# Weights laid out by the host so that each partition reads one contiguous run

## The chip, the cores and the metric

The kernel runs on one core of a Trainium2 chip. The metric is the device time of one execution in microseconds (us); what the host does before the launch is not in it. A core has TensorE (matmuls, "PE" in the rows, "PEld" for its weight loads), VectorE (DVE), ScalarE (ACT), GpSimd (POOL) and SyncE (SP), which issues most DMAs. Sixteen DMA engines serve all queues of the core.

## The reference, cut to what matters

Two layers of a diffusion backbone over 256 latent and 256 context tokens of width 1024, all in fp32. Each layer has a modulated input projection into three token mixers, a merge and a layer norm, then a mixture of 64 experts with eight per token and a shared expert, and a second layer norm.

```python
h = x * (1.0 + m[1]) + m[0]                      # m from s_c @ w_mod[l] + b_mod[l]
q, k, v, lx, lg, z, xbc, dt, gates = split(h @ w_in)   # 1024 x 7184
...
proj = einsum('blnk,nkd->blnd', ys, w_branch)    # three branches, 512 x 1024 each
out  = einsum('blnd,de->ble', g * proj, w_out)   # 1024 x 1024
x = layer_norm(DN_ALPHA * x + m[2] * mix, ln1_g[l], ln1_b[l])
...
# each of 64 experts e, on the tokens routed to it:
swiglu(h_pad[toks], w_up[e], w_down[e]) * ws     # w_up 1024 x 512, w_down 256 x 1024
```

The last layer needs the latent tokens only. The expert weights are 3 MB per expert, 192 MB per layer.

## The kernel before, in words

The kernel keeps 20 named slots of 1 MB in SBUF (8 KB in each of 128 partitions) and streams all weights through them in chunks of at most 1 MB. The contraction dimension is cut into blocks `k` of 128 rows; row `p` of each block goes to partition `p`. A chunk is therefore loaded with a view `(k p) f -> p k f`: each partition gets, for each `k`, one row piece of the matrix. The length of that piece in HBM is 1 KB for `w_mod`, `w_in` and `w_out` (256 columns of wider rows), 2 KB for `w_up` and `ws_up` (a full row of 512), 4 KB for `w_down` and `ws_down` (a full row of 1024), 512 B for `w_branch` (128 columns) and 256 B for the router weights and the lru blocks.

All these loads are issued by SP in program order, and a load waits until its slot is free. The order of the instructions is made while the program is built: a small cost model (`Plan`) decides which pieces of side work are put between the main matmuls.

- Start: `mod_load` (line 340) issues eight `w_mod` chunks behind the two loads of x and ctx, then come the first `w_in` chunks. From these and x the modulated input is built, split into a high and a low part.
- Mixer stage of each layer: class `Main` (line 505) goes through 28 column blocks of `w_in` and 4 of `w_out`. `load` fetches into two slots, `split` makes high and low parts with ACT and DVE, and TensorE multiplies. `mod_gen` loads the other `w_mod` chunks beside that. In `mixer` (line 546) the lru blocks are loaded by eight DMAs per layer, the dt columns of `w_in` by one, and at the merge `load_wb` (line 838) fetches 24 chunks of `w_branch`, in layer 0 through one buffer.
- Expert stage, `sublayer2` (line 1059): the router's result is sorted, so that experts come in order of their number of tokens. Experts are packed into units of up to 128 rows by a fixed list (46 units in layer 0). Each expert has three chunks, two halves of `w_up` and `w_down`. `fill` (line 1306) issues loads for the next chunks as long as slots of the ring are free (nine, later more in layer 0; eleven and later more in layer 1); `used` gives slots back after the last matmul on them and calls `fill` again. In layer 0 the tokens of a unit are fetched three units ahead with an indirect DMA from POOL (`gather`), and the results are added to one of two accumulators in HBM, in turn, by another (`scatter`). Layer 1 selects and combines tokens on TensorE instead and uses no indirect DMA. `overflow` (line 1640) is a loop for experts with more tokens than the list allows for.
- The helper `fold` (line 83) only reshapes the columns of a view. All engine instructions are recorded under one helper line, L149.

Of the kernel before, what the change touches and what calls it, by code (L numbers as in the profile page):

```python
# [18 lines left out]
P = 128  # L19
D = 1024  # L20
KD = D // P
# [3 lines left out]
DEPTH = 2  # L25
NE = 64
# [5 lines left out]
C_Q, C_K, C_V, C_LX, C_LG, C_Z, C_XBC, C_DT, C_G = 0, 512, 1024, 1536, 2048, 2560, 3072, 4096, 4112  # L32
# [198 lines left out]
def tile_kernel(ctx: ExitStack, tc: tile.TileContext, A: dict, out: bass.AP):  # L231
# [107 lines left out]

    def mod_load(lc, w):  # L340
        l, c = lc
        SP.dma_start(w, A["w_mod"][l, :, c * 256:(c + 1) * 256].rearrange("(k p) f -> p k f", p=P))

    def mod_rows(w, i=0):
        p = bank("tr")
# [65 lines left out]
    p = bank("tr")  # L411
# [93 lines left out]
    class Main:  # L505
# [3 lines left out]
        def load(self, upto):  # L509
            while self.nl < min(upto + 1, len(self.cols)):  # L510
                i = self.nl
                w = slot(self.l, f"WR{i % 2}", (KD, 256))
                nm, c0 = self.cols[i]
                SP.dma_start(w, A[nm][self.l, :, c0:c0 + 256].rearrange("(k p) f -> p k f", p=P))
                self.raw[i] = w
                self.nl += 1

# [28 lines left out]
    def mixer(l, main, order, hT, pre, late):  # L546
# [11 lines left out]
        ya, yb, ysp = qT, u[:, :, :TL], {}  # L558
        bd = slot(l, "M1", (2, 2, 256), off=1024)
        for i, nm in enumerate(("lru_wa", "lru_wi")):  # L560
            for d in range(2):
                src = A[nm][l, d].rearrange("(c two) k j -> two k c j", two=2)
                for h in range(2):
                    SP.dma_start(bd[h * 64:(h + 1) * 64, i, d, :].rearrange("p (c j) -> p c j", c=4), src[h])

        def xt(n):
            return xA[:, n, :] if n < 4 else xB[:, n - 4, :]
# [270 lines left out]
        def load_wb(i):  # L838
            if i >= 24 or i in wb:
                return  # L840
            br = (1, 2, 0)[i // 8]
            wb[i] = raws[i % len(raws)]
            SP.dma_start(wb[i], A["w_branch"][l, br, :, (i % 8) * P:(i % 8 + 1) * P].rearrange("(k p) f -> p k f", p=P))

        def split_wb(i):
            hi, lo = [view(tt.get(9 + 2 * (i % 2) + h, F32R), 0, (4, P)) for h in range(2)]
# [27 lines left out]
        for i, (kind, arg) in enumerate(order):  # L874
# [11 lines left out]
            elif kind == "xbc":  # L886
                if arg == 3:
                    steps()
                if arg == 0:
                    wd = view(tt[8], 0, (KD, 32))  # L890
                    V.memset(wd, 0.0)
                    SP.dma_start(wd[:, :, :16], A["w_in"][l, :, C_DT:C_DT + 16].rearrange("(k p) f -> p k f", p=P))
                for j in range(2):
                    n = 2 * arg + j
                    begun = state.pop((arg, j), None)
# [163 lines left out]
    def sublayer2(l, mg, wo, R):  # L1059
# [11 lines left out]

        def load(name, src, shape):
            w = slot(l, name, shape)
            SP.dma_start(w, src.rearrange("(k p) f -> p k f", p=P))
            return w


# [3 lines left out]
        posm = view(tt[10], 0, (NE, nb))  # L1081
        valw = fold(tt[11].bitcast(BF16)[:, :NE * nb * 3], (NE, nb, 3))
        wr = view(tt[8], 0, (KD, NE))
        SP.dma_start(wr, A["w_router"][l].rearrange("(k p) e -> p k e", p=P))
        rb = wk.tile([P, 256], F32, name="rbias", tag="rb", bufs=1)[:, :NE]
        SP.dma_start(rb, row_bc(A["router_bias"][l], NE))
        SHW = ("WR0", "WR1", "WL1")
# [218 lines left out]
        def fill(limit=len(chunks)):  # L1306
            while pos[0] < min(limit, len(chunks)):
                if not free:
                    return
                r, i = c = chunks[pos[0]]  # L1310
                if r >= fixed and not perm:
                    return
                if not last and pos[0] >= len(chunks) - HOLD and free[0] in ("M0", "M1"):
                    held.append(free.pop(0))
                    if len(held) == 2:
                        mains[1].start()
                    continue
                if r >= fixed and r not in reg:
                    reg[r] = nc.values_load(perm["row"][0:1, r:r + 1], engines=[mybir.EngineType.SP], min_val=0,
                                            max_val=NE - 1, skip_runtime_bounds_check_because="a permutation of 0..63")  # L1320
                e = slice(r, r + 1) if r < fixed else bass.ds(reg[r], 1)
                src = A["w_up"][l, e, i * 512:(i + 1) * 512, :] if i < 2 else A["w_down"][l, e]
                place[c] = free.pop(0)
                W[c] = slot(l, place[c], (4, 512) if i < 2 else (2, D))
                SP.dma_start(W[c], src.rearrange("o (k p) f -> p (o k) f", p=P))
                pos[0] += 1

        def used():
# [7 lines left out]

        load_x(0)
        load_x(1)
        shw += [load(n, A["ws_up"][l, h * 512:(h + 1) * 512, :], (4, 512)) for h, n in enumerate(SHW[:2])]
        if last:  # L1340
            fill(2)
        z = tt[2]
# [297 lines left out]
        def overflow(t):  # L1640
# [7 lines left out]
            with tc.For_i(0, nu) as i:  # L1648
                r = nc.values_load(eui[0:1, bass.ds(i, 1)], min_val=0, max_val=NE - 1)
                e = nc.values_load(eui[0:1, bass.ds(i + nu_max, 1)], min_val=0, max_val=NE - 1)  # L1650
                wu = [slot(l, n, (4, 512)) for n in spare[:2]]
                wd = slot(l, spare[2], (2, D))
                for h in range(2):
                    SP.dma_start(wu[h], A["w_up"][l, bass.ds(e, 1), h * 512:(h + 1) * 512, :]
                                 .rearrange("o (k p) f -> p (o k) f", p=P))
                SP.dma_start(wd, A["w_down"][l, bass.ds(e, 1)].rearrange("o (k p) f -> p (o k) f", p=P))
                pcol = wk.tile([P, nb + 1, 1], F32, name="pcol", bufs=1)
                pcol, bse = pcol[:, :nb], pcol[:, nb]
                V.tensor_copy(pcol, posm[:, bass.ds(r, 1), :].rearrange("p o b -> p b o"))
                V.tensor_copy(bse, eu[:, bass.ds(i, 1)])  # L1660
                V.tensor_scalar(pcol, pcol, bse, None, op0=OP.subtract)
                vw = wk.tile([P, nb, 3], BF16, name="vw", bufs=1)
                V.tensor_copy(vw, valw[:, bass.ds(r, 1), :, :].rearrange("p o b c -> p (o b) c"))
                OH = view(tt[8], 0, (nb, P))
                V.tensor_tensor(OH, col_i[:, None, :P].to_broadcast([P, nb, P]), pcol.to_broadcast([P, nb, P]),
                                op=OP.is_equal)
                bf = fold(tt[6].bitcast(BF16)[:, :nb * P], (nb, P))
                V.tensor_copy(bf, OH)
                select(NUN, bf, lambda b: vw[:, b, :], [slice(0, P)])
                if not last:  # L1670
                    gather(idx[NUN][0], X1, slice(0, P))
                xt_ = [XT(t, h) for h in range(2)]
                for h in range(2):
                    p = bank("tr")
                    if last:
                        rows_T(p, h, OH, P)
                    else:
                        for k in range(4):
                            PE.transpose(p[:, k * P:(k + 1) * P], X1[:, (4 * h + k) * P:(4 * h + k + 1) * P], ident)
                    S.activation(xt_[h], p.rearrange("p (k n) -> p k n", k=4), AF.Copy)  # L1680
                p = bank("mm")
                for k in range(KD):
                    PE.matmul(p, xt_[k // 4][:, k % 4, :], wu[k // 4][:, k % 4, :], start=k == 0, stop=k == KD - 1)
                a = swiglu_act(p)
                p = act_T(a, "tr")
                S.activation(a[:, 256:], p[:, :256], AF.Copy)
                aT = fold(a[:, 256:], (2, P))
                if last:
                    sv = tt[9][:, :256]
                    V.tensor_scalar(sv, col_i, toks[NUN], None, op0=OP.is_equal)  # L1690
                for h in range(2):
                    c = slice(h * 512, (h + 1) * 512)
                    p = bank("mm")
                    for k in range(2):
                        PE.matmul(p, aT[:, k, :], wd[:, k, c], start=k == 0, stop=k == 1)
                    S.activation(y[:, c], p, AF.Copy, scale=wcs[NUN])
                    if last:
                        V.tensor_mul(y[:, c], y[:, c], FR["m5"][0][:, c])
                        for b in range(2):
                            PE.matmul(acc_ps[2 * b + h], sv[:, b * P:(b + 1) * P], y[:, c], start=False, stop=False)  # L1700
                if not last:
                    G.indirect_dma_start(out=accs[0][:, :],
                                         out_offset=bass.IndirectOffsetOnAxis(ap=idx[NUN][0][:, :1], axis=0),
                                         in_=y, in_offset=None, bounds_check=TL + P - 1, oob_is_err=True,
                                         compute_op=OP.add)
# [160 lines left out]
    order += [("lg", 0), ("lg", 1)] + [("g", (1, i)) for i in range(4)]  # L1866
    order[-2:-2] = [("z", 0), ("z", 1)]
    order += [("g", (2, i)) for i in range(4)] + [("g", (0, i)) for i in range(4)]
    cols = [("w_in", C_G + a[0] * 1024 + a[1] * 256 if k == "g" else CO[k][0] + a * 256) for k, a in order]
    cols += [("w_out", q * 256) for q in range(4)]  # L1870


    mains = [Main(l, cols) for l in range(DEPTH)]
# [175 lines left out]
    return np.concatenate([np.cos(ang), np.sin(ang)], axis=-1).astype(np.float32)  # L2049


# [19 lines left out]
```

## Time and profile before

| | us |
|---|---|
| median of 3 runs | 2451.94 |
| lowest and highest | 2448.26, 2453.66 |
| the profiled execution, its own time | 2449.11 |
| its span, first to last instruction | 2447.2 |
| TensorE busy | 2215.5 (91%) |
| VectorE, ScalarE, GpSimd busy | 1047.5, 699.6, 477.7 |
| moved by DMA | 605.24 MB in 348050 packets |

Times in the rows are us from the start of the span. A DMA share is the time that packets took, over 16 engines; it can exceed 1 a little, since packets on one engine overlap. In rows of waits the columns are the waiting engine with what it writes, what it waited for, the total in us, how many times, and the longest. In timelines they are start, duration, engine, line, operation, operands, count, and in brackets the idle time before it with what ended it.

### The profile page before, as it was taken

To read this page: it belongs to the slowest core of one execution; us is meant where nothing else is said; L and a number is where in the kernel's file an instruction comes from. 1 tells how busy PE (TensorE), PEld (TensorE's weight loads), DVE (VectorE), ACT (ScalarE), POOL (GpSimd) and SP (SyncE) were. 2 spreads that over 40 slices of the span, in tenths; PEclk is the share of its full clock that TensorE was granted. 3 is DMA by queue.
4 is the path that set the end of the run, shared out by engine and by line. 5 is a ranking of instruction groups with operands and counts; after the bars stand their busy time and mean duration, and the time that the engine had idled before them with its cause. 6 is when DMAs were issued, how large, how long until landed. Compare 5 with 4: busy or idle time off the path is not lost. (4 is left out here: it accounts for less than half of the span.)

```text
span 2447.2 us, 37548 instructions
## 1 busy us (share of the span) xinstructions
PE 2215.5 (91%) x14847; PEld 1386.1 (57%) x14847; DVE 1047.5 (43%) x2315; ACT 699.6 (29%) x1268; POOL 477.7 (20%) x402
## 2 busy tenths in 40 slices
PE   6999999999879899999998849998997899999997
PEld 4778767777844333333333228786995444554553
DVE  4656455533653222322222156666665222333333
ACT  3465356323211111111111124666541111111111
POOL 0223202011222222223232144340212000000000
PEclk8999999999979999999999969999998999999999
DMA  9443434464649999999999942213566799999994
GB/s 287 152 129 107 138 108 129 154 202 131 244 178 277 362 350 341 354 338 345 337 336 346 366 150 88 69 52 99 164 217 223 264 350 391 380 396 394 393 393 159
DMA packets 348050, 605.24 MB, mean 247 GB/s; under 512 B 24552, under 2 KB 164160, under 8 KB 347872
## 3 DMA queue, kind: packets, MB, share of 16 engines
q1 hardware_dynamic: 332440, 560.97, 65.1%
q0 software_dynamic: 13952, 41.57, 7.0%
q8 instruction: 118, 1.93, 0.3%
q14 instruction: 60, 0.49, 0.1%
q10 hardware_dynamic: 1480, 0.27, 0.1%
HBM read 576.54 MB, written 31.06 MB: 248 GB/s over the span
## 5 line engine op out<-in xcount | busy, mean ns | idle before, releaser
L149 PE MATMUL mm<-s,t 128*32 128x512 f32 (+3 forms) x4320 | 673.4, 572 | 39.8 <-DMA s<-in_w_up_dram 36.3
L149 PE MATMUL mm<-s,s 128*128 128x256 f32 (+1 forms) x3488 | 564.4, 320 | 13.1 <-DVE tm L149 8.1
L149 PEld LDWEIGHTS mm<-s,s 128*128 128x128 f32 x3488 | 491.7, 193 | 71.8 <-issue 19.1
L149 PEld LDWEIGHTS mm<-s,t 128*32 128x32 f32 (+2 forms) x4320 | 262.8, 128 | 383.4 <-issue 306.5
L149 DVE TENSOR_TENSOR tm<-tm,mm 128x256 f32<-128x256 f32 (+3 forms) x194 | 85.7, 442 | 582.8 <-ACT tm L149 533.8
L149 ACT ACTIVATE tm<-mm 128x256 f32<-128x256 f32 (+3 forms) x155 | 65.1, 421 | 745.8 <-PE mm L149 736.7
L149 DVE TENSOR_TENSOR s<-s,s 128x1024 fp32r<-128x1024 f32 (+5 forms) x164 | 195.1, 1232 | 53.3 <-ACT s L149 49.9
L149 PE MATMUL sd<-s,tm 128*32 128x512 f32 (+2 forms) x1112 | 184.6, 633 | 26.2 <-DMA s<-in_w_down_dram 25.3
L149 POOL DMA_INDIRECT acc<-s,si x77 | 111.0, 1441 | 481.2 <-ACT t L149 246.8
L149 PE MATMUL sd<-s,s 128*128 128x512 f32 (+4 forms) x768 | 181.8, 451 | 12.3 <-ACT t L149 11.2
L149 ACT ACTIVATE s<-s 128x1024 fp32r<-128x1024 f32 (+4 forms) x170 | 150.6, 940 | 13.8 <-PE sd L149 6.1
L149 PEld LDWEIGHTS tr<-t,s 128*128 128x128 f32 x1024 | 125.4, 198 | 43.1 <-issue 42.1
L149 PEld LDWEIGHTS sd<-s,s 128*128 128x128 f32 (+2 forms) x768 | 110.6, 186 | 68.0 <-issue 33.4
L149 PEld LDWEIGHTS sd<-s,tm 128*32 128x32 f32 (+2 forms) x1112 | 54.9, 123 | 148.3 <-issue 117.5
L149 PE MATMUL tr<-t,s 128*128 128x128 f32 (+1 forms) x1024 | 133.5, 285 | 0.4 <-DVE t L149 0.4
L149 POOL TENSOR_TENSOR s<-s,tm 128x512 f32<-128x512 f32 (+1 forms) x52 | 64.0, 1232 | 320.2 <-ACT tm L149 158.9
L149 PE MATMUL mm<-s,tm 128*32 128x512 f32 (+1 forms) x760 | 109.1, 606 | 12.6 <-ACT tm L149 10.0
L149 ACT ACTIVATE t<-tr 128x512 f32<-128x512 f32 (+6 forms) x115 | 62.0, 544 | 197.3 <-PE tr L149 197.0
L149 PE MATMUL tr<-ident,s 128*128 128x128 f32 (+2 forms) x568 | 84.6, 294 | 33.9 <-DVE s L149 23.0
L149 POOL TENSOR_TENSOR t<-t,mhalf 128x2 f32<-128x2 f32 x1 | 0.7, 709 | 572.5 <-DVE t L149 572.5
L149 PEld LDWEIGHTS tr<-ident,s 128*128 128x128 f32 (+2 forms) x568 | 68.2, 151 | 76.1 <-issue 46.1
L149 ACT ACT_TABLE_LOAD x63 | 80.8, 1283 | 39.7 <-PE mm L149 13.6
(256 smaller groups left out, 2205.9 us busy)
## 6 DMA issues: line engine op xcount, KB each, us to landing
s<-in_w_up_dram SPq DMA_DIRECT2D x256, 1024.0 KB
s<-in_w_down_dram SPq DMA_DIRECT2D x128, 1024.0 KB
s<-in_w_in_dram SPq DMA_DIRECT2D x56, 1024.0 KB
s<-in_w_mod_dram SPq DMA_DIRECT2D x48, 1024.0 KB
t<-in_w_branch_dram SPq DMA_DIRECT2D x32, 256.0 KB
s<-in_w_out_dram SPq DMA_DIRECT2D x8, 1024.0 KB
acc<-t SPq DMA_DIRECT2D x4, 1280.0 KB
s<-in_ws_up_dram SPq DMA_DIRECT2D x4, 1024.0 KB
```

The source lines that it names most:

```text
L149: r = f(*a, **k)
```

## The change

The host reorders the large weights before the launch, so that what one partition needs of a chunk is contiguous in HBM: a chunk of 1 MB is then 128 runs of 8 KB. All of `w_mod`, `w_in`, `w_out`, `w_up`, `w_down`, `ws_up` and `ws_down` are loaded as 8 KB runs; `w_branch` in 2 KB runs, the router weights in 2 KB, the dt columns (an array `w_dt` of their own) in 512 B, the lru blocks in 2 KB. The lru blocks are loaded by two DMAs per layer instead of eight. What lands in SBUF, and every other instruction, is the same.

```diff
     def mod_load(lc, w):
-        SP.dma_start(w, A["w_mod"][l, :, c * 256:(c + 1) * 256].rearrange("(k p) f -> p k f", p=P))
+        SP.dma_start(w, fold(A["w_mod"][l, c], (KD, 256)))
...
                 nm, c0 = self.cols[i]
-                SP.dma_start(w, A[nm][self.l, :, c0:c0 + 256].rearrange("(k p) f -> p k f", p=P))
+                SP.dma_start(w, fold(A[nm][self.l, c0], (KD, 256)))
...
         for i, nm in enumerate(("lru_wa", "lru_wi")):
-            for d in range(2):
-                src = A[nm][l, d].rearrange("(c two) k j -> two k c j", two=2)
-                for h in range(2):
-                    SP.dma_start(bd[h * 64:(h + 1) * 64, i, d, :].rearrange("p (c j) -> p c j", c=4), src[h])
+            SP.dma_start(bd[:, i], fold(A[nm][l], (2, 256)))
...
-            SP.dma_start(wb[i], A["w_branch"][l, br, :, (i % 8) * P:(i % 8 + 1) * P].rearrange("(k p) f -> p k f", p=P))
+            SP.dma_start(wb[i], fold(A["w_branch"][l, br, i % 8], (4, P)))
...
-                    SP.dma_start(wd[:, :, :16], A["w_in"][l, :, C_DT:C_DT + 16].rearrange("(k p) f -> p k f", p=P))
+                    SP.dma_start(wd[:, :, :16], fold(A["w_dt"][l], (KD, 16)))
...
-        SP.dma_start(wr, A["w_router"][l].rearrange("(k p) e -> p k e", p=P))
+        SP.dma_start(wr, fold(A["w_router"][l], (KD, NE)))
...
-                src = A["w_up"][l, e, i * 512:(i + 1) * 512, :] if i < 2 else A["w_down"][l, e]
+                src = A["w_up"][l, e, i] if i < 2 else A["w_down"][l, e]
                 place[c] = free.pop(0)
                 W[c] = slot(l, place[c], (4, 512) if i < 2 else (2, D))
-                SP.dma_start(W[c], src.rearrange("o (k p) f -> p (o k) f", p=P))
+                SP.dma_start(W[c], src.rearrange("o p (k f) -> p (o k) f", k=W[c].shape[1]))
...
+def _tiles(a, rows, cols):
+    *lead, r, c = a.shape
+    a = a.reshape(*lead, r // (rows * P), rows, P, c // cols, cols)
+    n = len(lead)
+    a = a.transpose(*range(n), n, n + 3, n + 2, n + 1, n + 4)
+    return a.reshape(*lead, r // (rows * P) * (c // cols), P, rows * cols)
...
+    for n in ("w_mod", "w_out"):
+        a[n] = _tiles(a[n], KD, 256)
+    a["w_branch"] = _tiles(a["w_branch"], 4, P)
+    for n in ("w_up", "ws_up"):
+        a[n] = _tiles(a[n], 4, 512)
+    for n in ("w_down", "ws_down"):
+        a[n] = _tiles(a[n], 2, D)[..., 0, :, :]
```

The loads in `overflow`, the shared expert's and the column indices in `cols` change in the same way.

## Rows read from the trace of the kernel before

**Rows 1.** The page, DMA over the span in 40 slices: busy tenths, rate.

```profile
DMA  9443434464649999999999942213566799999994
GB/s 287 152 129 107 138 108 129 154 202 131 244 178 277 362 350 341 354 338 345 337 336 346 366 150 88 69 52 99 164 217 223 264 350 391 380 396 394 393 393 159
```

**Rows 2.** Busy time by stage: stretch, length, engines, PEclk, DMA share, GB/s.

```profile
0.00:44.00 44.00, 23.36 (x196) 15.09 (x197) 13.12 (x44) 12.69 (x25) 1.38 (x10) 0.87 0.97 313
44.00:718.00 674.00, 632.53 (x3955) 501.46 (x3954) 371.13 (x765) 278.71 (x496) 146.08 (x128) 0.96 0.46 148
718.00:1428.00 710.00, 635.03 (x4277) 250.24 (x4275) 189.04 (x550) 103.11 (x201) 186.03 (x153) 0.95 1.01 335
...
1900.00:2045.00 145.00, 134.04 (x804) 66.72 (x808) 40.61 (x106) 18.49 (x37) 0.00 (x0) 0.96 0.88 326
2045.00:2405.00 360.00, 346.94 (x2601) 179.69 (x2592) 117.44 (x314) 54.61 (x103) 0.00 (x0) 1.00 1.04 392
```

**Rows 3.** TensorE's waits from 718 to 1428 us.

```profile
PE mm L149 <- DMA s<-in_w_up_dram: 29.4, 11, 5.8
PE sd L149 <- DMA s<-in_w_down_dram: 25.3, 10, 6.0
```

**Rows 4.** TensorE's waits from 2045 to 2405 us.

```profile
PE mm L149 <- DMA s<-in_w_up_dram: 1.7, 2, 1.6
```

**Rows 5.** TensorE's waits from 1900 to 2045 us.

```profile
PE mm L149 <- DMA s<-in_w_up_dram: 5.2, 4, 1.7
```

**Rows 6.** Timeline of TensorE in layer 0's expert stage.

```profile
892.07 7.07 PE L149 MATMUL mm<-s,t 128*32 128x512 f32 x64
...
903.93 7.07 PE L149 MATMUL mm<-s,t 128*32 128x512 f32 x64
...
1317.44 1.05 PE L149 MATMUL mm<-s,t 128*32 128x512 f32 x4
...
1330.18 5.13 PE L149 MATMUL mm<-s,t 128*32 128x512 f32 x28 [5.76 <-DMA s<-in_w_up_dram]
1340.12 7.07 PE L149 MATMUL mm<-s,t 128*32 128x512 f32 x64
```

**Rows 7.** DMA queue of the weights, 61 to 540 us: packets, MB, share.

```profile
q1 hardware_dynamic: 70866, 65.78, 43.5%
```

**Rows 8.** The same queue from 2110 to 2400 us.

```profile
q1 hardware_dynamic: 48119, 113.85, 103.9%
```

**Rows 9.** The same queue from 10 to 35 us.

```profile
q1 hardware_dynamic: 7995, 8.06, 100.9%
```

**Rows 10.** Weights' and POOL's queues, 750 to 1405 us.

```profile
q1 hardware_dynamic: 80056, 189.59, 80.6%
q0 software_dynamic: 12016, 35.89, 23.2%
```

**Rows 11.** Timeline of the start, TensorE and ACT.

```profile
12.90 1.94 PE L149 MATMUL tr<-s,sT 128*32 128x256 f32 x16 [9.40 <-DMA s<-in_w_mod_dram]
...
39.95 2.00 ACT L149 ACTIVATE s<-s 128x1024 fp32r<-128x1024 f32 x2 [2.73 <-DMA s<-in_w_in_dram]
...
43.72 12.41 PE L149 MATMUL sd<-s,s 128*128 128x512 f32 x48
```

**Rows 12.** ACT's wait for w_branch in all; TensorE's timeline behind one.

```profile
ACT t L149 <- DMA t<-in_w_branch_dram: 48.8, 11, 6.8
...
608.25 3.02 PE L149 MATMUL mm<-s,t 128*128 128x512 f32 x12 [0.79 <-ACT tm L149]
```

**Rows 13.** Timeline of SP's queue at the lru blocks.

```profile
43.89 3.32 SPq L149 DMA_DIRECT2D s<-in_lru_wa_dram  x4
...
52.61 0.56 SPq L149 DMA_DIRECT2D s<-in_w_in_dram  x1
```

**Rows 14.** Gathers: issue to landing (us); scatters: count, KB, median landing.

```profile
DMA to landing us min/median/max: 2.3/8.1/10.9
...
acc<-s,si POOLq DMA_INDIRECT x77, 7.7
```

More of the change, by code (lines that the diff above doesn't have):

```diff
@@ L1073, in load @@
             w = slot(l, name, shape)
-            SP.dma_start(w, src.rearrange("(k p) f -> p k f", p=P))
+            SP.dma_start(w, fold(src, shape))
             return w
@@ L1338, in sublayer2 @@
         load_x(1)
-        shw += [load(n, A["ws_up"][l, h * 512:(h + 1) * 512, :], (4, 512)) for h, n in enumerate(SHW[:2])]
+        shw += [load(n, A["ws_up"][l, h], (4, 512)) for h, n in enumerate(SHW[:2])]
         if last:
@@ L1653, in overflow @@
                 for h in range(2):
-                    SP.dma_start(wu[h], A["w_up"][l, bass.ds(e, 1), h * 512:(h + 1) * 512, :]
-                                 .rearrange("o (k p) f -> p (o k) f", p=P))
-                SP.dma_start(wd, A["w_down"][l, bass.ds(e, 1)].rearrange("o (k p) f -> p (o k) f", p=P))
+                    SP.dma_start(wu[h], A["w_up"][l, bass.ds(e, 1), h].rearrange("o p (k f) -> p (o k) f", k=4))
+                SP.dma_start(wd, A["w_down"][l, bass.ds(e, 1)].rearrange("o p (k f) -> p (o k) f", k=2))
                 pcol = wk.tile([P, nb + 1, 1], F32, name="pcol", bufs=1)
@@ L1868, in tile_kernel @@
     order += [("g", (2, i)) for i in range(4)] + [("g", (0, i)) for i in range(4)]
-    cols = [("w_in", C_G + a[0] * 1024 + a[1] * 256 if k == "g" else CO[k][0] + a * 256) for k, a in order]
-    cols += [("w_out", q * 256) for q in range(4)]
+    cols = [("w_in", 16 + a[0] * 4 + a[1] if k == "g" else CO[k][0] // 256 + a) for k, a in order]
+    cols += [("w_out", q) for q in range(4)]
     mains = [Main(l, cols) for l in range(DEPTH)]
@@ L2049, in _rope_table, with _layouts @@
     return np.concatenate([np.cos(ang), np.sin(ang)], axis=-1).astype(np.float32)
+def _tiles(a, rows, cols):
[4 more added lines that the diff above has]
+    return a.reshape(*lead, r // (rows * P) * (c // cols), P, rows * cols)
+def _layouts(inputs):
+    import numpy as np
+    a = {n: np.asarray(inputs[n]) for n in _INS}
+    w = a["w_in"]
+    a["w_in"] = np.concatenate([_tiles(w[:, :, :C_DT], KD, 256), _tiles(w[:, :, C_G:], KD, 256)], axis=1)
+    a["w_dt"] = _tiles(w[:, :, C_DT:C_G], KD, 16)[:, 0]
+    for n in ("w_mod", "w_out"):
+        a[n] = _tiles(a[n], KD, 256)
+    a["w_branch"] = _tiles(a["w_branch"], 4, P)
+    a["w_router"] = _tiles(a["w_router"], KD, NE)[:, 0]
+    for n in ("w_up", "ws_up"):
+        a[n] = _tiles(a[n], 4, 512)
+    for n in ("w_down", "ws_down"):
+        a[n] = _tiles(a[n], 2, D)[..., 0, :, :]
+    for n in ("lru_wa", "lru_wi"):
+        a[n] = a[n].reshape(DEPTH, 2, 4, 2, 64, 64).transpose(0, 3, 4, 1, 2, 5).reshape(DEPTH, P, 512)
+    a["c_rope"] = _rope_table()
+    return {n: np.ascontiguousarray(x) for n, x in a.items()}
 def kernel(**inputs):
@@ L2060 @@
     arrays, A = {}, {}
-    for name in _INS + ["c_rope"]:
-        a = _rope_table() if name == "c_rope" else _np.ascontiguousarray(inputs[name])
+    for name, a in _layouts(inputs).items():
         arrays[f"in_{name}_dram"] = a
```

## The prediction

> **What bounds the kernel now.** I read the utilisation lines first, then busy time by stage, then the waits of TensorE in the stages where DMA is full, and last the timelines that show how a wait is passed on. The utilisation lines [rows 1] show that the DMA engines are not uniformly loaded: full in the first slice, about half loaded in both mixer stages, full without a break for some 11 slices of layer 0's expert stage (around 345 GB/s) and for about 7 of layer 1's (around 393 GB/s). By stage [rows 2] the picture sharpens. In the mixer stages (44 to 718 us) TensorE is busy 632.5 of 674 us and DMA 46%: weights arrive early and nobody on the path waits for them. In layer 0's expert stage (718 to 1428 us) the DMA share is 1.01 while TensorE has 75 idle us, of which 29.4 and 25.3 us end with the landing of an expert's up or down weights [rows 3]. In layer 1's, DMA is just as full (1.04 from 2045 to 2405 us), but TensorE is busy 347 of 360 us and waits 1.7 us for weights [rows 4]: it is fed just in time, so faster weights buy next to nothing there. Only its opening (1900 to 2045 us) shows 5.2 us of such waits [rows 5].
>
> The timeline says that layer 0's expert stage is DMA-bound as a whole and not at a few places. A unit that waits for nothing takes 903.93 - 892.07 = 11.86 us; the one from 1317.44 to 1340.12 takes 22.68, with a wait of 5.76 us for up weights and slower matmuls behind it [rows 6]. Such units recur until the stage's end: the waits of [rows 3] are 21 in number. The 46 units of the unit list at 11.86 would be 546 us of a stage of 710. A ring that runs dry again and again, with no pause in the DMA engines, means that what sets the end is the bytes' own time.
>
> **The price of a longer run.** The change alters no byte count. It alters the length of the contiguous piece: 1 KB (w_in, w_mod, w_out), 2 KB (w_up), 4 KB (w_down), 512 B (w_branch) all become 8 KB, w_branch 2 KB. So I need engine time per packet as a function of its size, from windows in which one size prevails. Method A takes two quiet windows. From 61 to 540 us: 70866 packets, 65.78 MB, 43.5% of 16 engines over 479 us [rows 7], that is 208.4 x 16 / 70866 = 47.0 ns for a mean of 928 B. From 2110 to 2400 us: 48119 packets, 113.85 MB, 103.9% of 290 us [rows 8], that is 100.2 ns for 2366 B. A line through them: 12.7 ns plus 37.0 ns per 1000 B. It gives 50.6, 88.4, 164 and 315 ns for 1, 2, 4 and 8 KB. Method B takes the two crowded windows, in which other queues push in. From 10 to 35 us: 7995 packets, 8.06 MB, 100.9% [rows 9], 50.5 ns for 1008 B; from 750 to 1405 us: 80056 packets, 189.59 MB, 80.6% of 655 us [rows 10], 105.5 ns for 2368 B. The line: 9.7 ns plus 40.4 per 1000 B, so 51.1, 92.5, 175 and 341 ns. The 8 KB figures are extrapolations: no row shows a weight run of that length. One engine's part of an expert (3 MB over 16) costs 64 x 88.4 + 16 x 164 = 8.29 us now and 24 x 0.315 = 7.57 after by A, a fall of 8.7%; by B 8.72 to 8.18, 6.2%.
>
> [...]
>
> **Part by part.**
> - Expert loads of layer 0 (the ring's `fill`). The weight queue's 80.6% of 655 us is 528 us of engine time [rows 10]. 8.7% of it is 46, 6.2% is 33; the engines run at a share of 1.04 when full (80.6 + 23.2 and a rest), so 44 or 32 us of clock time. I take the middle, -38, since this stage has B's contention but its packets are mostly A's sizes. It is all on the path as long as TensorE still waits afterwards: 38 is under the 54.7 us of named waits. What is late next is still the weights: I expect some 20 us of named waits to remain.
> - Start. The first matmul on w_mod comes at 12.90 us, and ACT waits until 39.95 us for the first w_in chunk, whose split precedes the long matmuls at 43.72 [rows 11]. Nine 1 MB chunks of 1 KB runs stand in that queue. Each costs 64 x 50.6 = 3.24 us and then 8 x 0.315 = 2.52 (A, -0.72) or 3.27 to 2.73 (B, -0.54): -6.5 or -4.9, I take -6.
> - Layer 1's opening: 5.2 us of waits [rows 5] over about 60 us of full DMA, of which 8.7% is 5.2; between -2 and -6, I take -4. The rest of that stage: 0, hidden by TensorE itself, at most the 1.7 us [rows 4].
> - Merge of layer 0: ACT waits 48.8 us for w_branch chunks, but the matmuls behind stand idle for 0.79 us at a time [rows 12], so -1 (0 to -3).
> - Mixer loads of w_in and w_mod, the router and shared weights: 0. TensorE's own work covers them (632.5 of 674 us); without that cover each chunk would save 0.5 to 0.7 us.
> - The lru blocks: eight issues hold SP's queue from 43.89 us, and the next w_in issue follows only at 52.61 [rows 13]; two issues replace them. TensorE works 12.41 us from 43.72, so 0; the w_in chunk behind merely goes out earlier. No wait is added anywhere, nothing is moved past another queue's work, and the order of instructions should stay.
> - Relayout on the host is outside the device time.
>
> Sum: -38 - 6 - 4 - 1 = -49 us. The profiled execution took 2449.1 us with a span of 2447.2, 2.8 below the median of the three runs, 2451.9; I set the sum against it: 2400. Bounds of the terms: -32 - 5 - 2 - 0 = -39 (2410) and -44 - 6.5 - 6 - 3 = -59 (2390).
>
> **Rivals.**
> - The change does only half of what it says: the 8 KB runs are cut into 4 KB pieces on the way. For: nothing in the trace shows a longer weight packet. Against: the queues show none that was cut either, 2 and 4 KB go whole. An expert costs 48 x 164 = 7.88 (A, -5.0%) or 48 x 175 = 8.41 (B, -3.6%): -25 or -18 in layer 0, -5 at the start, -3 elsewhere: 2416 to 2423.
> - The length of a run does not matter at these sizes, and the small windows were dearer for their contention: nothing moves, 2449. For: in no window do two sizes stand alone. Against: both pairs give a constant of 10 to 13 ns per packet. [...]
> - TensorE takes over: half of the named waits turn into waits for ACT and DVE. Gain 27 in layer 0, time 2411. Against: most units wait for weights alone.
> - Slower: the gathers and scatters of layer 0 starve. They run on another queue (23.2% of the engines [rows 10]) beside the weights. A gather lands in 2.3 us at best and in 8.1 at the median, a scatter in 7.7 [rows 14], so the neighbours add about 5.8. Scatters alternate between two accumulators, and one waits for the one before it on the same accumulator; 77 scatters in 46 units make 31 units with two. If the added 5.8 grew with the packet, 3.15 times, a scatter would land in 7.7 + 5.8 x 2.15 = 20.2 us, and the stage would need 31 x 20.2 + 15 x 11.86 = 804 us against the 655 in which DMA is full: +149, and 2449 + 149 - 11 = 2587. It decides where 31 x L + 178 = 655 - 38, at L = 14.2 us. Against: I expect one 8 KB packet to stand between two of the 8 scatter packets of an engine instead of one of 2 to 4 KB, 8 x 0.215 = 1.7 us more, about 9.5. [...]
>
> **How the numbers follow.** Forecast 70%, runs cut 12%, TensorE takes over 5%, nothing moves 8%, scatters starve 5%. A measurement of this kernel can tell about 0.2%, 5 us. The first three are faster (0.87), the fourth is the same (0.08), the last slower (0.05). The range starts at 2380, 10 below the better bound for the extrapolation, and reaches over the cut runs with the same allowance, to 2432; outside are the last two cases and some 6% of the others' tails.
>
> **What would show it.** In the profile after: packets fall from 348050 to near 100000, most of them of 8 KB. Packet time in layer 1's full window (by packets, MB and share) near 315 ns for 8 KB; 341 would be B, and 4 KB pieces would show in the count. Layer 0's expert stage about 38 us shorter, its rate up from 345 to some 365 GB/s at a share still above 1, TensorE's named waits down from 54.7 to about 20. Layer 1's full stretch as long as before, its DMA share down to about 0.95. The first long matmuls near 38 us. Gather and scatter landing near 9.5 us; above 14 the prediction is wrong in sign. Wrong in size it would be if 8 KB packets took under 300 or over 350 ns, or if TensorE's idle time in layer 0 moved to ACT and DVE.

## The result and the profile after

The median falls from 2451.94 to 2415.26 us (2408.79 to 2422.18), a ratio of 0.984 with a 95% interval of 0.981 to 0.987: 36.7 us, where 49 to 52 were forecast. One more execution of before took 6918 us and is left out of its median. The profiled execution of after is the slowest of its four, 2422.18 us with a span of 2420.2, so the two profiles differ by 27.0.

The page of after, DMA over the span in 40 slices, and the weight queue (packets, MB, share), beside [rows 1]:

```profile
DMA  7433333454648999999999942212455789899992
GB/s 293 155 126 108 122 126 124 146 193 142 228 170 295 367 360 347 353 356 350 343 352 354 375 140 89 70 53 101 166 211 221 275 359 421 367 421 420 405 417 84
DMA packets 107218, 605.24 MB, mean 250 GB/s; under 512 B 18216, under 2 KB 18560, under 8 KB 42784
q1 hardware_dynamic: 91608, 560.97, 60.1%
```

The bytes are those of before, in 107218 packets instead of 348050. Layer 1's slices rise to 420 GB/s, layer 0's only to some 355. The same by stage, in the columns of [rows 2]:

```profile
718.00:1428.00 710.00, 635.34 (x4284) 250.72 (x4282) 199.60 (x560) 102.52 (x201) 192.59 (x157) 0.96 0.98 344
...
2045.00:2405.00 360.00, 345.87 (x2600) 180.03 (x2598) 119.39 (x315) 56.02 (x105) 0.00 (x0) 1.00 0.89 366
...
2300.00:2350.00 50.00, 48.83 (x359) 26.42 (x352) 16.06 (x40) 7.66 (x15) 0.00 (x0) 1.00 1.01 421
```

The stretches are those of before, and layer 1 lies some 27 us earlier in them. So the fall of the DMA share from 1.04 to 0.89 behind 2045 us is not room in the engines: the last line shows them full, at 1.01 and 421 GB/s, and the loads simply end at some 2370 us, 35 us before the stretch does. In layer 0's expert stage they are full too. TensorE's waits from 718 to 1410 us, beside [rows 3], fell from 54.7 to 40.0 us and not to 20:

```profile
PE mm L149 <- DMA s<-in_w_up_dram: 22.0, 15, 3.1
PE sd L149 <- DMA s<-in_w_down_dram: 18.0, 11, 4.3
```

I measure the stage from the first matmul on expert weights to the end of TensorE's wait for the accumulators that follows the last expert. The two rows of before and then of after, TensorE's timeline:

```profile
718.54 8.96 PE L149 MATMUL mm<-s,t 128*128 128x512 f32 x16
...
1435.61 5.40 PE L149 MATMUL mm<-s,ident 128*128 128x512 f32 x8 [13.01 <-DMA s<-acc]
```

```profile
718.35 7.93 PE L149 MATMUL mm<-s,t 128*128 128x512 f32 x14
...
1416.70 6.04 PE L149 MATMUL mm<-s,ident 128*128 128x512 f32 x8 [13.77 <-DMA s<-acc]
```

717.1 us became 698.4: -18.7, where -38 was forecast. From there to the end of the span it is 1011.6 before and 1003.5 after. The start, TensorE's timeline of after beside [rows 11]:

```profile
23.16 1.93 PE L149 MATMUL tr<-s,sT 128*32 128x256 f32 x16 [2.59 <-DMA s<-in_w_mod_dram]
...
40.70 3.76 PE L149 MATMUL sd<-s,s 128*128 128x512 f32 x8
```

The long matmuls begin at 40.70 instead of 43.72. The 3.0 us are not seen at the experts (718.35 against 718.54): short stretches of a lower granted clock fall at other places in the two profiles (0.50 of full speed from 194 to 200 us in after, 0.82 from 116 to 122 us in before, each beside 1.00 in the other). From 190 to 207 us the granted clock is 0.70 in after and 1.00 in before, and the lead is lost there.

Last the queues in the two full windows, 750 to 1385 us (weights, POOL) and 2105 to 2250 (weights), beside [rows 10] and [rows 8]:

```profile
q1 hardware_dynamic: 26082, 188.89, 77.5%
q0 software_dynamic: 12012, 35.89, 23.9%
...
q1 hardware_dynamic: 8485, 60.74, 100.9%
```

In layer 1 an 8 KB packet takes 100.9% x 145 us x 16 engines over some 7415 packets = 316 ns, as method A said. In layer 0 it is 77.5% x 635 x 16 over some 23060 = 341 ns, method B's number. Below I use such rows as engine time per MB (share times window over MB): 2.409 us in layer 1 and 2.605 in layer 0, against 2.646 and 2.785 before.

### The profile page after: what moved, and what is told of

Read it like the earlier page. It is cut to its first block, busy times and chain, and to the rows that moved or that the text cites. A ratio compares the mean times of both kernels' runs of the same rounds, so it can differ in the third digit from the quotient of the medians.

```text
span 2420.2 us, 37534 instructions
## 1 busy us (share of the span) xinstructions
PE 2208.3 (91%) x14847; PEld 1388.6 (57%) x14847; DVE 1049.0 (43%) x2315; ACT 699.1 (29%) x1268; POOL 477.6 (20%) x402
## 2 busy tenths in 40 slices
DMA packets 107218, 605.24 MB, mean 250 GB/s; under 512 B 18216, under 2 KB 18560, under 8 KB 42784
## 5 line engine op out<-in xcount | busy, mean ns | idle before, releaser
L149 DVE TENSOR_TENSOR tm<-tm,mm 128x256 f32<-128x256 f32 (+3 forms) x194 | 85.7, 442 | 572.6 <-ACT tm L149 518.9
```

The source lines that it names most:

```text
L149: r = f(*a, **k)
```

## Experiments

**1 and 2. The two halves of the change by themselves.** Experts only (the layouts and loads of w_up and w_down), then everything but these ("the rest only"); the part of the edit shown is the second's.

```diff
-                src = A["w_up"][l, e, i] if i < 2 else A["w_down"][l, e]
+                src = A["w_up"][l, e, i * 512:(i + 1) * 512, :] if i < 2 else A["w_down"][l, e]
```

> The new layout for the routed experts' w_up and w_down alone; all other weights are read as before. Theory (most of the gain is layer 0's expert stage, which stays DMA-bound; the rest of the new layout is hidden): the two expert stages give the 18.7 and about 8 us that separate the two profiles there, so about 2424 us, a ratio near 0.989, and with the run-to-run scatter that the four runs of the changed kernel show (2408.8 to 2422.2) anything from 2415 to 2430. Rival (gain spread over all loads, since mixer loads also give TensorE a smoother supply): under half of the 37 us, about 2435. In its profile the stretch from the first layer-0 up matmul to the wait for the accumulators should be near 698 us as after the change, the long matmuls at the start should begin at 43.7 as before.

> The new layout for everything but the routed experts' w_up and w_down. Theory: only the start gains, 3.0 us by the two profiles (first long matmuls 40.7 instead of 43.7), and nothing in the mixer stages, so 2449 +- 4, a ratio of 0.998 to 1.000. The prediction's term was 6 to 7 us (2445). Rival (gain spread over all loads): 10 to 20 us, a ratio of 0.992 to 0.996.

Measured beside a before of 2454.06 us: experts only 2423.31 (ratio 0.987, 0.985 to 0.990), the rest only 2447.62 (0.997, 0.995 to 0.999, where 0.998 to 1.000 was expected). The stage took 697.4 us with the experts alone (717.94 to 1415.35) and 720.6 with the rest alone. So -31 of the change comes from the experts, -6 from all else, and the two add up to the whole.

**3. The hole at the start.** In after the weight queue nearly stops for about 2.5 us while small packets of another queue (q10, ACT's) pass. DMA of after from 15 to 20 us, rate in 40 slices and the two queues:

```profile
GB/s 655 328 459 463 270 606 262 529 459 139 225 97 39 38 8 7 7 7 7 7 7 7 9 10 11 11 43 103 404 116 121 55 206 320 78 0 66 207 272 393
...
q1 hardware_dynamic: 111, 0.78, 51.1%
q10 hardware_dynamic: 768, 0.10, 11.8%
```

The engines themselves are busy under a tenth from 16.75 to 17.9 us. The three loads behind these packets fill `sm`: a row of 8 or 16 numbers broadcast to 128 partitions. The edit moves them behind other loads of the same queue.

```diff
-        eng.dma_start(sm[:, 0:16], row_bc(A["ssd_dt_bias"][l], 16))
...
+        eng.dma_start(sm[:, 0:16], row_bc(A["ssd_dt_bias"][l], 16))
```

> The changed kernel, with three small broadcast loads of layer 0 (dt bias, a_log and d, one row to all 128 partitions each) issued on ACT's queue at a later step, behind the parameter rows' transpose, instead of right behind those rows. Theory (the start did not gain its 6 us because the weight queue stands nearly still for some 2.5 us, from 16.2 to 18.6 us, while 752 to 768 small packets of the other queue pass): the hole goes, the fourth chunk's matmuls begin at about 20.5 instead of 23.16, the long matmuls at about 38.3 instead of 40.7, and the whole is 2 to 3 us under the changed kernel, hardly visible in the time (0.1%). Rival (the start is held by TensorE, ACT and DVE working off the chunks, not by the hole): the hole goes or stays, and the long matmuls still begin near 40.7. If the hole stays, the rope table's load or the rows themselves make it.

Measured: the 2.59 us wait is gone, and from 13 to 20 us the two queues together keep 369 GB/s. Its timeline:

```profile
27.72 1.07 PE L149 MATMUL tr<-s,sT 128*32 128x256 f32 x16 [0.68 <-DMA s<-in_w_mod_dram]
...
38.83 3.76 PE L149 MATMUL sd<-s,s 128*128 128x512 f32 x8
```

The long matmuls start at 38.83, 4.9 us before those of before. But before has such a hole too, and no run takes it out there, so the 4.9 us are not the price of the packets alone. The total, 2416.56 us (2412.33 to 2420.40), can't be told from after's.

**4. Expert weights in 4 KB runs.** The host cuts each partition's 8 KB in two, which lie apart in HBM.

```diff
-                SP.dma_start(W[c], src.rearrange("o p (k f) -> p (o k) f", k=W[c].shape[1]))
+                SP.dma_start(W[c].rearrange("p (g k) f -> p g (k f)", g=2), src.rearrange("o g p f -> p (o g) f"))
```

> The changed kernel with the routed experts in runs of 4 KB: two per partition and chunk, each half chunk contiguous; w_down thus reads runs as long as before the change, w_up twice as long as before and half as long as after it. Theory (each packet costs a fixed part, of which some 4 ns pass beside the next packet whatever its length, so that net it is about 9 ns + 37 per 1000 B): full stretch of layer 1 at about 409 GB/s, between 394 and 420; a share of about 102.5%; layer 0's full stretch at 350 GB/s and its gain about 60% of the 18.7 us; whole time about 2425. Rival (the prediction's constant of 12.7 ns with a fixed 4% overlap): 399 x 1.04 = 415 GB/s in layer 1. Rival (only the number of DMA packets beside the scatters counts, their length harms): layer 0 gains as much or more with 4 KB than with 8, 18.7 us or over.

Measured: 2423.47 us (2421.75 to 2432.46), the stage 698.3 us (720.90 to 1419.24), as long as with 8 KB, so that the gain is 18.8 us: the expected 60% of 18.7 failed, and the second rival's 18.7 or more came out. The stage's end, then its weight queue in layer 0 (750 to 1385 us) and in layer 1 (2105 to 2250):

```profile
1419.24 5.99 PE L149 MATMUL mm<-s,ident 128*128 128x512 f32 x8 [13.76 <-DMA s<-acc]
...
q1 hardware_dynamic: 49027, 189.20, 78.8%
...
q1 hardware_dynamic: 15345, 59.10, 102.2%
```

In layer 1 the packets follow the price list (2.507 us per MB, 409 GB/s against 420). In layer 0 it is 2.645. A MB costs 0.138 us more in layer 0 than in layer 1 here, and the same 0.138 in before, but 0.196 in after. Over 189 MB that is 26 us of engine time for 2 to 4 KB runs and 37 for 8 KB. Something in layer 0 takes back what the second doubling gives.

**5. The price list by itself.** Loads alone, in eight phases.

> No computation of the reference: only loads. Eight phases of 48 chunks of 1 MB into twelve slots in turn, from one array's weights laid out in runs of 1, 2, 4 and 8 KB; four phases alone, then the same four with a chain of scatters into two accumulators and gathers beside them (128 rows of 4 KB each, as in layer 0's expert stage). Theory (net cost per packet, since about 4 ns of its busy time pass beside the next one): alone 350, 389, 410 and 421 GB/s in the full part of each phase, with shares of about 1.08, 1.05, 1.025 and 1.013. The prediction's way (busy time over a fixed 1.04) would give 432 for 8 KB. Beside the scatters, by theory, a weight packet of 8 KB takes 335 to 345 ns of engine time instead of 312 to 316 and the total for 8 KB is 2 to 4% above the total for 2 KB. Rival (scatters don't lengthen weight packets): packet times beside them equal those alone, and the total gains 5 to 6% from 2 to 8 KB.

The weight queue in the four phases without other work (1, 2, 4 and 8 KB), windows of 75, 100, 100 and 95 us:

```profile
q1 hardware_dynamic: 25898, 26.11, 110.1%
...
q1 hardware_dynamic: 19476, 38.68, 105.2%
...
q1 hardware_dynamic: 10625, 40.96, 102.6%
...
q1 hardware_dynamic: 5615, 40.05, 101.4%
```

That is 348, 387, 410 and 422 GB/s, each within 1% of what was expected. The share above 100% is the overlap of neighbouring packets on an engine: 10.1 of 110.1% of 51 ns, 5.2 of 105.2% of 86 ns, 2.6 of 102.6% of 164 ns, 1.4 of 101.4% of 314 ns (the last two by the mean of the window's 4 KB or 8 KB packets), 4 to 5 ns every time. In these windows it is a fixed time per packet and not a fixed share. From 1 to 8 KB the rate rises by 21% (348 to 422 GB/s).

The other half of the expectation failed. Beside scatters and gathers with 8 KB runs (1160 to 1300 us):

```profile
q1 hardware_dynamic: 4803, 34.95, 60.5%
q0 software_dynamic: 4424, 16.16, 42.5%
```

An 8 KB packet took 60.5% x 140 x 16 over 4266 = 318 ns and no more, where it took 314 alone. So indirect transfers of 128 rows hardly lengthen the weight packets of 8 KB. Counted by their bytes, the two queues passed nearly equal numbers of packets at both run lengths: 4814 weight packets beside 4417 indirect ones with 2 KB runs (765 to 855 us), 4266 beside 3945 with 8 KB. So beside such a queue longer packets brought the weight queue a larger share of the engines, 60.5% with 8 KB where it was 30.3% with 2 KB.

**6. Layer 0 without indirect transfers.**

> The changed kernel without layer 0's gathers and scatters: the tokens of a unit are left at zero and its results are not added, so that the routed experts of layer 0 contribute nothing; matmuls, loads and their order stay. Theory (layer 0's expert stage is bound by the bytes of both queues, 24% of the engine time of which is the indirect ones'): it becomes TensorE's, with 46 units at 11.86 us and the shared expert's pieces, about 60 to 75 us shorter than the 698 us after the change, named waits for weights under 10 us; the weight packets of 8 KB return to 312 to 318 ns from 340. Rival (the stage is held by TensorE's order of work and the named waits are only stolen from other waits): under 30 us shorter.

Measured in one run: 2339.64 us, the stage 618.7 (from 719.05), 79.7 less than after and more than the 60 to 75 expected. TensorE waits for no weights in it. So 698 us are set by DMA, both queues together, and TensorE's own floor lies near 619. The weight queue (740 to 1320 us, then 1280 to 1320) and the stage's end:

```profile
q1 hardware_dynamic: 26581, 192.57, 85.7%
...
q1 hardware_dynamic: 2305, 16.75, 100.5%
...
1337.70 6.57 PE L149 MATMUL mm<-s,ident 128*128 128x512 f32 x8 [10.75 <-DMA s<-acc]
```

The packet time expected did not come out: 85.7% x 580 x 16 over 23507 is 338 ns, much as in after. But here the engines are not full (333 GB/s), and where they are, in the second window, an 8 KB packet takes 100.5% x 40 x 16 over 2045 = 314 ns at 420 GB/s. In the packet records of the first window the median is 309 ns, and one packet in twenty takes over 418. So the mean of a window that is not full can mislead; why those few are long stays open.

**7 and 8. Is it which rows are gathered?** Loads alone beside gathers of consecutive, spread, scattered and identical rows; and the kernel after with consecutive rows in place of the chosen tokens.

```diff
+            V.tensor_tensor(gi[:n], row_i[:n], tr_[:n], op=OP.add)
...
-                for si, (_, _, _, c, m) in zip(idx[t], units[t]):
+                for si, (_, _, _, c, m) in zip(gix[t], units[t]):
```

> A kernel of loads alone: eight phases of 48 chunks of 1 MB, four with 8 KB runs and then four with 4 KB runs. Beside each phase 16 gathers of 128 rows of 4 KB are issued. The rows of a gather are, phase by phase: 128 consecutive ones, every fourth of 512, scattered ones (37 times the index, modulo 512), and 128 times the same one. Open is why an 8 KB weight packet takes about 340 ns in layer 0's expert stage and 316 in layer 1's, while beside consecutive rows in the loads alone it took some 318. Theory (which rows are fetched matters): beside scattered rows an 8 KB packet takes 380 to 480 ns while the gathers run and a gathered row over 200, and the rate there is below 330 GB/s; beside consecutive rows 310 to 320, 160 and over 400 GB/s; the 4 KB packet is lengthened by half as much as the 8 KB one. Rival (something else in that stage does it): the phases with consecutive, spread and scattered rows agree within 3%.

> The kernel after, but the gathers of layer 0 fetch consecutive rows of the token array instead of the tokens that the router chose (padding is skipped as before), so layer 0's experts work on the wrong tokens; the scatters still go where they went. One short VectorE instruction per unit is added, two where it has two experts. Theory (the scattered rows of the gathers lengthen the weight packets beside them): the weight queue's time per MB in layer 0's full window falls from 2.61 to about 2.45 us and layer 0's expert stage from 698 to 650 to 675 us; time 2365 to 2392. Rival (other causes): stage 695 to 701, time 2410 to 2422.

The theory fell both times. The loads alone, rate in 40 slices, and the end of the kernel's stage:

```profile
GB/s 323 419 418 422 422 420 418 419 422 422 419 418 418 422 422 418 419 419 422 420 410 409 410 410 409 410 410 409 410 410 409 410 410 409 410 410 409 411 409 345
...
1417.81 5.69 PE L149 MATMUL mm<-s,ident 128*128 128x512 f32 x8 [14.34 <-DMA s<-acc]
```

The loads keep 418 to 422 GB/s beside every pattern with 8 KB runs and 409 to 411 with 4 KB. The kernel took 2413.78 us (2411.91 to 2422.47), its stage 695.5 (from 722.32), its weight queue 78.1% of 635 us for 190.33 MB, 2.606 us per MB as after.

**9 and 10. Is it how a gather's rows are cut?** What loads alone and kernel still differed in: the kernel gathers per expert, into 32 to 128 partitions, the loads alone always into all 128. Experiment 9 gathers the same rows in four cuts; experiment 10 is the kernel after with one gather per unit.

```diff
+            V.tensor_copy(si, trash)
             V.scalar_tensor_tensor(si[:n], ids[:n], -1.0, tr_[:n], op0=OP.add, op1=OP.add)
...
-                for si, (_, _, _, c, m) in zip(idx[t], units[t]):
-                    gather(si, Xb[t % len(Xb)], slice(c, c + m))
+                gather(idx[t][0], Xb[t % len(Xb)], slice(0, P))
```

> A kernel of loads alone: eight phases of 48 chunks of 1 MB, four with 8 KB runs and then four with 4 KB runs. Beside each phase consecutive rows of 4 KB are gathered, 2048 in all, into partitions cut in four ways: 128 rows at a time, twice 64 (partitions 0 to 63 and 64 to 127), four times 32, and 64 at a time always into partitions 0 to 63. [...] Rival (the cut doesn't matter): the four ways agree within 3%.

> The kernel after, but each unit of layer 0 fetches its tokens with one gather over all 128 partitions instead of one per expert over that expert's partitions; indices of rows that are not wanted are out of bounds and are skipped, as padding was. One short VectorE instruction per unit is added; some 30 of the 77 gathers go. Nothing is left out. Theory (cut gathers lengthen the weight packets): the weight queue's time per MB in layer 0's full window falls from 2.61 to 2.41 to 2.50 us, layer 0's expert stage from 698 to 655 to 685 us, time 2372 to 2403. Rival (the cut doesn't matter): stage 690 to 701 by the spared instructions of POOL's queue at most, time 2407 to 2422.

Experiment 9 with 8 KB runs, beside whole gathers (40 to 85 us) and beside twice 64 rows (185 to 235 us):

```profile
DMA packets 3306, 18.83 MB, mean 418 GB/s; under 512 B 360, under 2 KB 360, under 8 KB 1656
...
q1 hardware_dynamic: 1850, 13.52, 72.1%
q0 software_dynamic: 1456, 5.31, 29.5%
```

```profile
DMA packets 2731, 14.44 MB, mean 289 GB/s; under 512 B 422, under 2 KB 422, under 8 KB 1514
...
q1 hardware_dynamic: 1367, 9.97, 70.4%
q0 software_dynamic: 1364, 4.47, 31.5%
```

Beside cut gathers an 8 KB packet takes 70.4% x 50 x 16 over 1217 = 463 ns instead of 72.1% x 45 x 16 over 1650 = 315, and a gathered row 231 instead of 164. Four times 32 rows give 296 GB/s: twice as many gathers, and no lower a rate, so it is not their number. With 4 KB runs it is 410 against 282: the packet goes from 164 to 235 ns, half as much more for half the bytes, so both lengths end at the same rate. (The fourth cut gave 349 and 343; its gathers did not run throughout.) So the loads beside a gather into 64 or 32 partitions are slowed with it; what holds the two up no row shows.

Experiment 10 took 2378.17 us (2374.71 to 2383.63), ratio to before 0.968 (0.966 to 0.971). Its weight queue in layer 0 (750 to 1350 us) and layer 1 (2070 to 2215 us), TensorE's waits for weights from 718 to 1370 us, and the stage's end:

```profile
DMA packets 38505, 226.91 MB, mean 378 GB/s; under 512 B 6334, under 2 KB 6334, under 8 KB 15350
q1 hardware_dynamic: 26282, 190.36, 76.9%
q0 software_dynamic: 12176, 35.89, 24.3%
...
q1 hardware_dynamic: 8485, 60.75, 100.9%
```

```profile
PE sd L149 <- DMA s<-in_w_down_dram: 17.3, 9, 4.3
...
PE mm L149 <- DMA s<-in_w_up_dram: 2.3, 4, 0.8
...
1379.29 6.02 PE L149 MATMUL mm<-s,ident 128*128 128x512 f32 x8 [13.62 <-DMA s<-acc]
```

The stage is 660.9 us (from 718.37), 37.5 less than after. 2.424 us per MB in layer 0 against 2.408 in layer 1: the surplus fell from 37 us to 3. The scatters are still cut by expert, and the 3 us hold whatever that costs the loads.

**11 and 12. Whole gathers with short runs.** The same edit in the kernel before, and in the kernel of experiment 4.

> The kernel before, with its short runs, but each unit of layer 0 fetches its tokens with one gather over all 128 partitions, as in the whole-gather version of the kernel after. Nothing is left out. Theory (the cut gathers ate part of the long runs' gain): the weight queue's time per MB in layer 0's full window falls from 2.78 to 2.66 to 2.72 us, the stage from 717 to 692 to 708 us, time 2427 to 2443; so that with whole gathers the long runs are worth 50 us or more (2378 against this), as the prediction had it, of which some 38 in layer 0. Rival 1 (a cut gather holds up long packets only): stage 712 to 718, time 2445 to 2454. Rival 2 (it costs the same bytes' time at every run length): stage 675 to 685, time 2410 to 2420, and the long runs stay worth 36.

> The kernel after with the experts' weights in runs of 4 KB and with whole gathers in layer 0. Nothing is left out. Theory (4 and 8 KB tied in layer 0 only because cut gathers hold both to the same rate): the stage is 5 to 15 us longer than the 661 of whole gathers with 8 KB, time 2384 to 2396. Rival (they tie for another reason): stage 658 to 664, time 2378 to 2385 (layer 1's opening is some 2 us longer in either case).

Weight queue of the first in layer 0 (750 to 1350 us), layer 1 (2075 to 2220 us) and its stage's end; then the stage's end of the second:

```profile
DMA packets 88120, 216.73 MB, mean 361 GB/s; under 512 B 6127, under 2 KB 6127, under 8 KB 88074
q1 hardware_dynamic: 76154, 180.98, 80.2%
q0 software_dynamic: 11920, 35.11, 23.4%
...
q1 hardware_dynamic: 23748, 56.96, 103.7%
...
1405.49 6.25 PE L149 MATMUL mm<-s,ident 128*128 128x512 f32 x8 [13.42 <-DMA s<-acc]
```

```profile
1391.58 6.60 PE L149 MATMUL mm<-s,ident 128*128 128x512 f32 x8 [13.49 <-DMA s<-acc]
```

Before with whole gathers: 2418.19 us (2412.52 to 2423.30), stage 687.5 (from 718.01), 2.659 us per MB. My theory (2427 to 2443, long runs then worth 50) fell; the time is in the range of the second rival, the stage 2.5 us above it. Cut gathers cost 29.6 us of stage with short runs and 37.5 with long ones, by one profile each. The same expert loads gave stages of 717.1 and 720.6 in before and the rest only, and of 695.5 to 698.4 in four kernels with 8 KB expert runs: after, experts only, experiments 3 and 8. So such a difference is known to some 4 us. With whole gathers the long runs are worth 26.6 us in the stage (687.5 to 660.9) and 40.0 in all. 4 KB with whole gathers: 2386.00 us (2383.44 to 2392.97), stage 669.6 (from 721.95), 8.7 longer than with 8 KB, as expected: the tie of experiment 4 was the cut gathers' doing.

| kernel | stage, us | median, us |
|---|---|---|
| before; 4 KB; after (cut gathers) | 717.1; 698.3; 698.4 | 2451.94; 2423.47; 2415.26 |
| the same with whole gathers | 687.5; 669.6; 660.9 | 2418.19; 2386.00; 2378.17 |
| after, consecutive rows | 695.5 | 2413.78 |
| after, no indirect transfers | 618.7 | 2339.64 |

## Why the prediction was right in sign and too large

**What bounds the kernel: right.** The gain of the largest term is in the stage and the queue that were named, experts alone bring -31 of -37, and without the indirect transfers the same stage falls to TensorE's own time. The router, shared, w_in and w_mod loads in the mixers moved nothing that the runs can tell.

**Layer 0, -38 forecast, -18.7 measured: the step that failed.** It has two faults.

The first is the step "the engines run at a share of 1.04 when full (80.6 + 23.2 and a rest), so 44 or 32 us of clock time". It took the overlap as a share that stays. It is 4 to 5 ns per packet (experiment 5), and with a third of the packets most of it goes: in the whole-gather pair, where contention is out of the way, the engine time of a MB falls by 8.8% (2.659 to 2.424), just method A's 8.7%, but the sum of the shares falls too, from 103.9 to 101.5%. What counts is the rate, 361 to 378 GB/s, +4.7%, 28 us over 600; the stage gave 26.6 where the step gave 44. The rows ahead of the prediction held it: [rows 8] alone is 3.9% of 100 ns.

The second is "I take the middle" between A and B. Layer 0 went by B alone: the engine time of a MB fell by 6.5% (2.785 to 2.605), where B said 6.2% and A 8.7%. I had read B's higher price as contention, and let it stand as a matter of packet size. It was the cut gathers, which hold 4 and 8 KB packets to the same 282 to 289 GB/s. They cost 0.126 us of engine time per MB with short runs (2.785 against 2.659) and 0.181 with long ones (2.605 against 2.424), and in the stage 26.6 became 18.7. That they were cut stood in the code, and the sum has no term for it.

**Start, -6 forecast, -3.0 measured.** Here too the chunks were priced by busy time. By the rates of experiment 5 (348 and 422 GB/s) a chunk of 1 MB takes 3.01 and 2.49 us, and nine of them save 4.7 us and not 6.5. The hole of 2.5 us was overlooked; without it after starts 4.9 us earlier than before, but what before would gain without its own is not shown, so the missing 1.7 us stay open.

**Layer 1, -4 forecast, -8.1 in the profiles.** Here the gain was larger, and "faster weights buy next to nothing there" was wrong. From the accumulators' wait to the end of the span, the kernels with short expert runs need 1011.6, 1011.2 and 1015.9 us (before, the rest only, before with whole gathers), those with long ones 999.6 to 1006.6 (eight kernels, the two with 4 KB runs among them; 1003.5 in after). That is some 10 us, and it belongs to the expert loads. The named waits hold only a part: 5.2 us in the opening [rows 5], of which 4.2 remain between 1890 and 2045 us, and 1.7 behind it [rows 4], of which none remain. Set side by side instruction by instruction, TensorE of before falls behind that of after by 3.4 us around the opening's waits, by 1.8 us between 2150 and 2195 us, where no wait for weights is named, and by 3.7 us between 2246 and 2275 us. In the last stretch 64 matmuls from 2254.44 us on take 10.3 us in before, 1.7 of them named waits, and 7.1 in after. Why they take longer than the named waits account for stays open.

**Merge, -1:** too small to be told apart in these runs. **Sum:** -18.7 - 8.1 - 0.2 up to the experts = -27.0 by the profiles, -36.7 by the medians; the runs of after spread over 13 us, and its profile is of the slowest. That the total lies no more than 12 to 15 us off the forecast is in part luck: layer 1 gave more than was forecast and made up for some of what layer 0 gave less.

**The rivals.** Runs cut into 4 KB: the page shows 107218 packets, so they were not, although the total of 2415 could hardly have told: that rival's range begins at 2416, and 4 KB runs of the experts took 2423. Nothing moves: false. TensorE takes over: it did not, 40 us of waits for weights remain. Scatters starve: their landing rose from 7.7 to 9.0 us and the gathers' from 8.1 to 10.6, near the 9.5 expected and under 14.2; the one weight packet between two of theirs, from which the 9.5 was worked out, was an assumption that no row ahead of the prediction shows, and the nearly equal numbers of packets in experiment 5 (4266 beside 3945 with 8 KB) agree with it. The contention that mattered was the reverse, the gathers holding up the weights (463 ns for an 8 KB packet instead of 315 in experiment 9).

Gathers' landing in after, and the scatters' with their count and median, beside [rows 14]:

```profile
DMA to landing us min/median/max: 2.3/10.6/13.2
...
acc<-s,si POOLq DMA_INDIRECT x77, 9.0
```

## What to carry to other kernels

Where a stage is bound by DMA, price a change of run length by the rate of a full window and not by busy time of packets: busy time counts the overlap, which was 4 to 5 ns per packet here and went away with the packets. Before pricing, look at what else moves in that stage: gathers into 64 partitions beside the loads held runs of 4 and 8 KB to one low rate (282 and 289 GB/s), and making them span all partitions was worth as much here (37 us) as the whole relayout.

## What the runs showed of the hardware

- Loads of 128 partitions alone ran at 348, 387, 410 and 422 GB/s in runs of 1, 2, 4 and 8 KB.
- Gathers into 64 or 32 partitions cut the total from 418 to 289 or 296 GB/s while they ran, and with 4 KB runs from 410 to 282 or 290; which rows a whole gather read, consecutive, spread, scattered or all the same, made no difference (418 to 422, with 4 KB runs 409 to 411).
- Beside a busy indirect queue the weight queue passed about as many packets as it (4814 beside 4417 at 2 KB, 4266 beside 3945 at 8 KB), so its share grew with its packets.
- Small packets from a second queue (768 of 130 B on average beside the weight queue's 111) left the weight queue almost no bytes for 2.5 us (0.08 MB from 16.2 to 18.6 us); with three of their loads issued later the two queues together kept 369 GB/s from 13 to 20 us.
